# Relative-position-bias softmax: the first two chunks loaded in pieces on two DMA queues

## The chip, the cores and the metric

The kernel runs on one core of a Trainium2 chip. The metric is the time of one execution on the device in microseconds (us); the median of several runs is compared. Before the change it is 1325.94 us (three runs, 1325.74 to 1336.57).

## What is computed

```python
# logits: (B=2, H=8, S=2112, S) fp32, rel_bias: (H, 33) fp32, max_rel = 16
rel_clipped = np.clip(pos[:, None] - pos[None, :], -max_rel, max_rel) + max_rel
bias = rel_bias[:, rel_clipped]
logits = logits + bias[None, :, :, :]
logits = logits - logits.max(axis=-1, keepdims=True)
exp = np.exp(logits)
return (exp / exp.sum(axis=-1, keepdims=True)).astype(np.float32)
```

Each row of 2112 numbers gets a bias that depends only on the head and on the clipped distance to the diagonal, and then a softmax. Input and output are 285.5 MB each, so 571 MB pass between the chip's main memory (HBM) and the core's own memory (SBUF).

## The kernel before, in words

One batch has 8 x 2112 = 16,896 rows, which is 132 (`RP`) for each of the 128 partitions. A **chunk** is 6 (`R`) rows of each partition, 128 x 12,672 fp32 numbers or 6.49 MB (6336 KB on the page). There are four chunk buffers, `X[0]` to `X[3]` (`NBUF = 4`): `X[0]` and `X[1]` carry two neighbouring groups of rows of batch 0, `X[2]` and `X[3]` the same groups of batch 1. The outer loop has 11 (`K`) turns of four chunks, 44 chunks in all. Every chunk is loaded once, worked on in place and stored from the same buffer.

Three engines and two DMA queues share the work, and the order on each is written by hand:

- **SyncE** (SP) issues the loads. Four loads come first, one for each buffer (line 97). Then a loop (line 99) waits for the store of a buffer (`st[m]`) and issues the next load into it.
- **VectorE** (DVE) first builds the bias. It clears a tile (line 120), waits for the small `rel_bias` load (`rb`, line 143), spreads the 33 values of its head over a band in a PSUM tile `F` (lines 144 to 168), and then enters its loop (line 222). At the head of each turn `window(k)` copies the strip of `F` that this turn needs into `F2` (line 172). For each chunk `add(m)` waits for the chunk (`ld[m]`) and does six fused passes, one for each row: add the bias, negate, and take the running minimum (line 186). After ScalarE has done the exponentials, `scale(m)` takes reciprocals (line 210) and multiplies four of the six rows (line 213).
- **ScalarE** (ACT) issues the load of `rel_bias` (line 122) when VectorE's clearing is done (`zero`). Then it does the six exponentials of a chunk with their sums (line 197), scales the other two rows (line 218), and issues the chunk's store (line 95) when all six rows are scaled (`scaled`).

Loads so go on SyncE's queue (q1 on the page), stores and the `rel_bias` load on ScalarE's queue (q10). Both queues feed the same 16 DMA engines. GpSimd makes two small index tables at the start and nothing else; TensorE does nothing.

Of the kernel before, what the change touches and what calls it, by code (L numbers as in the profile page):

```python
# [15 lines left out]
def kernel(  # L16
# [6 lines left out]
    nc = tc.nc  # L23
    P = 128
    B, H, S, S2 = logits.shape
# [3 lines left out]
    RP = H * S // P  # L29
# [4 lines left out]
    NBUF = 4  # L34
    R = 6
    M = NBUF // B
    G = M * R
# [6 lines left out]
    X = [io.tile([P, R * S], FP32, tag=f"X{b}", name=f"X{b}") for b in range(NBUF)]  # L44
# [22 lines left out]
    def view(t, offset, dims):  # L67
        return bass.AP(tensor=t.tensor, offset=t.offset + offset, ap=[[list(t.ap[0])[0], P]] + dims)

    def rows(t, k, m):  # L70
        return bass.AP(
            tensor=t.tensor, offset=t.offset + (m // M) * (H * S * S) + (m % M) * R * S + k * (G * S), ap=[[RP * S, P], [1, R * S]],
        )

    with tc.tile_critical(no_gpsimd_drain=True):  # L75
        ld = [nc.alloc_semaphore(f"ld{b}") for b in range(NBUF)]
        st = [nc.alloc_semaphore(f"st{b}") for b in range(NBUF)]
# [2 lines left out]
        scaled = nc.alloc_semaphore("scaled")  # L80
        inv = nc.alloc_semaphore("inv")
        rb = nc.alloc_semaphore("rb")
        zero = nc.alloc_semaphore("zero")
        idx = nc.alloc_semaphore("idx")
        dve = nc.alloc_semaphore("dve")

        def take(eng, sem, n):
            eng.wait_ge(sem, n).then_inc(sem, -n)  # L88

        def load(k, m):  # L90
            nc.sync.dma_start(out=X[m][:, :], in_=rows(logits, k, m)).then_inc(ld[m], 16)

        def store(k, m):
            take(nc.scalar, scaled, R)
            nc.scalar.dma_start(out=rows(out, k, m), in_=X[m][:, :]).then_inc(st[m], 16)

        for m in range(NBUF):
            load(0, m)
        with nc.Fori(0, K - 1, 1, engines=[ENG.SP]) as k:
            for m in range(NBUF):  # L100
# [5 lines left out]
        v = nc.vector  # L106
# [6 lines left out]
        def settle():  # L113
# [9 lines left out]
            out=bass.AP(tensor=F2.tensor, offset=F2.offset, ap=[[Q * step, P // Q], [1, H * W]]),  # L123
            in_=bass.AP(tensor=rel_bias.tensor, offset=rel_bias.offset, ap=[[0, P // Q], [1, H * W]]),
        ).then_inc(rb, 16)
        nc.gpsimd.iota(pid[:, :], pattern=[[0, 2]], base=0, channel_multiplier=1).then_inc(idx, 1)
        nc.gpsimd.iota(
            num, pattern=[[1, NB + 1]], base=0, channel_multiplier=0,
# [11 lines left out]
        for o, n, s, op in ((eq, NB, q, ALU.is_equal), (lt, NB, q, ALU.is_lt), (hsel, H, h, ALU.is_equal),  # L140
# [24 lines left out]
                           in_=view(reg, 1, [[1, NB - 1], [0, RP - W]])))  # L165
# [5 lines left out]
        def window(k):  # L171
            then(v.tensor_copy(out=F2[:, 0:SW], in_=F[:, bass.ds(RP - G - k * G, SW)]))  # L172
            settle()

        def row(m, i):
            return X[m][:, i * S : (i + 1) * S]

        def col(t, m, i, n=1):
            c = m * R + i
            return t[:, c : c + n]  # L180

        def add(m):
            take(v, ld[m], 16)
            for i in range(R):
                x = G - 1 - (m % M) * R - i
                v.tensor_tensor_reduce(  # L186
                    out=row(m, i), in0=row(m, i), in1=F2[:, x : x + S],
                    scale=-1.0, scalar=BIG, op0=ALU.add, op1=ALU.min, accum_out=col(nmax, m, i),
                ).then_inc(added, 1)
# [18 lines left out]
        def scale(m):  # L208
            take(v, expd, R)
            v.reciprocal(out=col(rec, m, 0, R), in_=col(tot, m, 0, R)).then_inc(inv, 1 if m < NBUF - 1 else NBUF + 1)  # L210
            scales_begin(v, m)
            for i in range(DV):
                v.tensor_scalar_mul(out=row(m, i), in0=row(m, i), scalar1=col(rec, m, i)).then_inc(scaled, 1)  # L213

        def scale_rest(m):
            scales_begin(nc.scalar, m)
            for i in range(DV, R):
                nc.scalar.activation(  # L218
                    out=row(m, i), in_=row(m, i), func=ACTF.Copy, scale=col(rec, m, i),
                ).then_inc(scaled, 1)  # L220

        with nc.Fori(0, K, 1, engines=[ENG.DVE]) as k:  # L222
            window(k)
            for m in range(NBUF):
                add(m)
                scale(m)
        with nc.Fori(0, K, 1, engines=[ENG.Activation]) as k:
            for m in range(NBUF):
                exps(m)
                scale_rest(m)  # L230
                store(k, m)
# [31 lines left out]
```

## Time and profile before

| what | before |
|---|---|
| median of three runs | 1325.94 us (1325.74, 1325.94, 1336.57) |
| span of the profiled execution | 1323.8 us; the two quick runs lie 1.9 and 2.1 us above it |
| VectorE, ScalarE busy | 866.2 us (65%), 757.2 us (57%) |
| DMA | 570.98 MB, mean 431 GB/s |
| DMA queue q1 (loads), q10 (stores) | packets take 50.0% and 49.8% of 16 engines' span |
| a chunk's load, issue to landing | 17.6 / 38.4 / 82.8 us (least, median, most) |
| a chunk's store, issue to landing | 59.0 us (median) |

The span runs from the first to the last instruction of the core. The profile gives no further time for the execution that it shows, so its own time is taken as its span and the 2.1 us by which the median run lies above it. Instruction times below are counted from the start of the span. "Issue to landing" is the time from the instruction that hands a transfer to its queue until its semaphore has fired; it contains the time for which the transfer stood behind others. An engine name with a q (SPq, ACTq, DVEq) is that engine's instruction sequencer, where waits and DMA issues sit.

### The profile page before, as it was taken

How to read it: one execution, taken by the hardware profiler on the slowest of the kernel's cores; microseconds unless marked ns; L12 is line 12 of the kernel's file. 1: busy time of each engine (PE TensorE's matmuls, PEld its weight loads, DVE VectorE, ACT ScalarE, POOL GpSimd, SP SyncE). 2: the span in 40 equal slices, each digit the busy share in tenths (PEclk: the TensorE clock that was granted, in tenths of full speed). 3: DMA queues.
4: the chain of work that ended last, by engine and by line, in shares of the span. 5: the costliest groups of instructions: out<-in, count | busy, mean ns of one | idle time of the engine just before them, and what ended most of it. 6: DMA issues, size and time to landing. Idle time of an engine off the chain costs nothing. (4 is left out here: it accounts for less than half of the span.)

```text
span 1323.8 us, 2109 instructions
## 1 busy us (share of the span) xinstructions
DVE 866.2 (65%) x781; ACT 757.2 (57%) x627; POOL 0.4 (0%) x6
## 2 busy tenths in 40 slices
DVE  6886666566766675576667666556766576566662
ACT  3776655556666555555656555555666565555663
POOL 0000000000000000000000000000000000000000
DMA  9999999999999999999999999999999999999998
GB/s 417 417 423 435 441 435 423 441 438 421 440 441 427 430 441 435 424 440 438 424 437 440 437 423 440 440 421 438 441 432 426 441 437 423 440 440 423 437 441 369
DMA packets 12682, 570.98 MB, mean 431 GB/s; under 512 B 1412, under 2 KB 1416, under 8 KB 1416
## 3 DMA queue, kind: packets, MB, share of 16 engines
q1 hardware_dynamic: 6336, 285.48, 50.0%
q10 hardware_dynamic: 6344, 285.48, 49.8%
q14 instruction: 2, 0.02, 0.0%
HBM read 285.48 MB, written 285.47 MB: 431 GB/s over the span
## 5 line engine op out<-in xcount | busy, mean ns | idle before, releaser
L197 ACT ACTIVATE X<-X,nmax 128x2112 f32<-128x2112 f32 x264 | 542.6, 2055 | 505.1 <-DVE nmax L186 472.4
L186 DVE CUSTOM_DVE_ANT_0 X<-X,F 128x2112 f32<-128x2112 f32 x264 | 605.2, 2354 | 319.1 <-DVEq L88 319.1
L213 DVE TENSOR_SCALAR X<-X,rec 128x2112 f32<-128x2112 f32 x176 | 220.3, 1315 | 2.8
L218 ACT ACTIVATE X<-X,rec 128x2112 f32<-128x2112 f32 x88 | 176.1, 2048 | 17.2 <-DVE rec L210 12.2
L210 DVE RECIPROCAL rec<-tot 128x6 f32<-128x6 f32 x44 | 8.4, 191 | 106.2 <-DVEq L88 106.2
L197 ACT ACTIVATION_READ_ACCUMULATOR X<-X,nmax 128x1 f32 x264 | 49.2, 186 | 0.0
L197 ACT ACT_TABLE_LOAD x11 | 14.1, 1283 | 22.6 <-ACTq L88 19.9
L172 DVE COPY F<-F 128x2123 f32 x11 | 26.0, 2361 | 0.5 <-DVEq L88 0.5
L186 DVE DVE_READ_ACCUMULATOR2_ANT nmax<- 128x1 f32 x264 | 21.6, 82 | 0.0
L144 DVE LOAD_MASK_SELECT F<-F x1 | 0.0, 14 | 6.2 <-DMA F<-in_rel_bias_dram 6.2
L164 DVE COPY F<-own 128x1485 f32<-128x1485 f32 x1 | 1.7, 1698 | 0.0
L120 DVE MEMSET F<- 128x264 f32 x1 | 0.3, 278 | 1.1 <-SPq L75 1.1
L142 DVE TENSOR_SCALAR Z<-rec,Z 128x16 f32<-128x16 f32 (+2 forms) x5 | 0.8, 233 | 0.1
L163 DVE TENSOR_TENSOR F<-F,own 128x528 f32<-128x528 f32 x1 | 0.7, 717 | 0.1
L160 DVE TENSOR_TENSOR F<-Z,own 128x528 f32<-128x528 f32 x1 | 0.7, 705 | 0.0
L150 DVE TENSOR_REDUCE own<-F 128x33 f32<-128x264 f32 x1 | 0.6, 609 | 0.1
L147 DVE TENSOR_TENSOR F<-F,Z 128x264 f32<-128x264 f32 x1 | 0.4, 429 | 0.1
L144 DVE STREAM_SHUFFLE F<-F 128x264 f32<-128x264 f32 x1 | 0.4, 442 | 0.0
L158 DVE SCALAR_TENSOR_TENSOR own<-Z,own 128x16 f32<-128x16 f32 x1 | 0.2, 235 | 0.2 <-DVEq L88 0.2
L155 DVE TENSOR_SCALAR own<-Z,own 128x16 f32<-128x16 f32 x1 | 0.2, 235 | 0.2 <-DVEq L88 0.2
L166 DVE COPY F<-own 128x115 f32<-128x115 f32 x1 | 0.3, 271 | 0.0
L168 DVE COPY F<-own 128x115 f32<-128x115 f32 x1 | 0.3, 271 | 0.0
(11 smaller groups left out, 1.6 us busy)
## 6 DMA issues: line engine op xcount, KB each, us to landing
X<-in_logits_dram SPq DMA_DIRECT2D x44, 6336.0 KB, 38.4
out_dram<-X ACTq DMA_DIRECT2D x44, 6336.0 KB, 59.0
F<-in_rel_bias_dram ACTq DMA_DIRECT2D x1, 4.1 KB
```

What stands on the lines that cost most here:

```text
L142: then(v.tensor_scalar(out=o, in0=num[:, 0:n], scalar1=s, scalar2=None, op0=op))
L144: then(v.stream_shuffle(out=T, in_=T, mask=[0] * Q))
L150: then(v.tensor_reduce(out=rbK, in_=view(F2, H * W, [[1, W], [W, H]]), axis=mybir.AxisListType.X, op=ALU.add))
L160: then(v.tensor_tensor(out=bands, in0=view(eq, 0, [[1, NB], [0, W]]), in1=view(rbK, W - 1, [[0, NB], [-1, W]]), op=ALU.mult))
L163: then(v.tensor_tensor(out=bands, in0=bands, in1=view(rest, 0, [[1, NB], [0, W]]), op=ALU.add))
L164: then(v.tensor_copy(out=view(F, C0 + W, [[RP, NB - 1], [1, RP - W]]), in_=view(reg, 1, [[1, NB - 1], [0, RP - W]])))
L172: then(v.tensor_copy(out=F2[:, 0:SW], in_=F[:, bass.ds(RP - G - k * G, SW)]))
L186: v.tensor_tensor_reduce(out=row(m, i), in0=row(m, i), in1=F2[:, x : x + S], scale=-1.0, scalar=BIG, op0=ALU.add, op1=ALU.min, accum_out=c ...
L197: nc.scalar.activation(out=row(m, i), in_=row(m, i), func=ACTF.Exp, scale=-1.0, bias=col(nmax, m, i), accum_out=col(tot, m, i),).then_inc( ...
L210: v.reciprocal(out=col(rec, m, 0, R), in_=col(tot, m, 0, R)).then_inc(inv, 1 if m < NBUF - 1 else NBUF + 1)
L213: v.tensor_scalar_mul(out=row(m, i), in0=row(m, i), scalar1=col(rec, m, i)).then_inc(scaled, 1)
L218: nc.scalar.activation(out=row(m, i), in_=row(m, i), func=ACTF.Copy, scale=col(rec, m, i),).then_inc(scaled, 1)
```

## The change

Only the first load of `X[0]` and of `X[1]` changes. Each is cut into two pieces, by rows of each partition:

| piece | rows of the chunk | queue | semaphore |
|---|---|---|---|
| chunk 0, first half | 0 to 2 | SyncE | `ld[0]` |
| chunk 0, second half | 3 to 5 | ScalarE, behind `rel_bias` | `head0` |
| chunk 1, first part | 0 to 4 | ScalarE, behind the piece above | `ld[1]` |
| chunk 1, last row | 5 | SyncE, between chunk 0's half and chunk 2 | `head1` |

VectorE waits for `head0` once, ahead of its loop and so ahead of the first `window` copy, and before every `add(1)` for `head1`, which stays at 16 once it is there. All other loads and all stores are as before.

```diff
+    def part(t, k, m, a, b):
+        return bass.AP(
+            tensor=t.tensor, offset=t.offset + (m // M) * (H * S * S) + ((m % M) * R + a) * S + k * (G * S),
+            ap=[[RP * S, P], [1, (b - a) * S]],
+        )
...
+        head0 = nc.alloc_semaphore("head0")
+        head1 = nc.alloc_semaphore("head1")
...
+        def load_part(eng, m, a, b, sem):
+            eng.dma_start(out=X[m][:, a * S : b * S], in_=part(logits, 0, m, a, b)).then_inc(sem, 16)
...
-        for m in range(NBUF):
+        HALF = R // 2
+        load_part(nc.sync, 0, 0, HALF, ld[0])
+        load_part(nc.sync, 1, R - 1, R, head1)
+        for m in range(2, NBUF):
             load(0, m)
...
         ).then_inc(rb, 16)
+        load_part(nc.scalar, 0, HALF, R, head0)
+        load_part(nc.scalar, 1, 0, R - 1, ld[1])
...
         def add(m):
             take(v, ld[m], 16)
+            if m == 1:
+                v.wait_ge(head1, 16)
...
+        v.wait_ge(head0, 16)
         with nc.Fori(0, K, 1, engines=[ENG.DVE]) as k:
             window(k)
```

What the change moves is seen at three places. ScalarE's instructions from its first DMA to its first exponential, before (F_62 is the tile F2; X_58 to X_61 are the four chunk buffers):

```order
L122 DMA F_62<-in_rel_bias_dram 4x264 [waits zero]
L88 UNCONDITIONAL_BRANCH
L227 UNCONDITIONAL_BRANCH
L197 ACT_TABLE_LOAD
L197 ACTIVATE X_58,tot<-X_58,nmax 128x2112 [waits added] x6
```

and now:

```order
L136 DMA F_62<-in_rel_bias_dram 4x264 [waits zero]
L102 DMA X_58<-in_logits_dram 128x6336
L102 DMA X_59<-in_logits_dram 128x10560
L96 UNCONDITIONAL_BRANCH
L246 UNCONDITIONAL_BRANCH
L215 ACT_TABLE_LOAD
L215 ACTIVATE X_58,tot<-X_58,nmax 128x2112 [waits added] x6
```

Two load pieces now stand between the `rel_bias` load and ScalarE's table load, and wait for nothing of their own. SyncE's issues ahead of its loop, and the first of the loop, before:

```order
L91 DMA X_58<-in_logits_dram 128x12672
L91 DMA X_59<-in_logits_dram 128x12672
L91 DMA X_60<-in_logits_dram 128x12672
L91 DMA X_61<-in_logits_dram 128x12672
L99 UNCONDITIONAL_BRANCH
L91 ISA [waits st0]
L91 DMA X_58<-in_logits_dram 128x12672
```

and now:

```order
L102 DMA X_58<-in_logits_dram 128x6336
L102 DMA X_59<-in_logits_dram 128x2112
L99 DMA X_60<-in_logits_dram 128x12672
L99 DMA X_61<-in_logits_dram 128x12672
L113 UNCONDITIONAL_BRANCH
L99 ISA [waits st0]
L99 DMA X_58<-in_logits_dram 128x12672
```

The first two issues have shrunk to three rows and one row; the rest stands as it stood. VectorE from the last piece of the bias to the first add, before:

```order
L168 COPY F<-own 128x115
L222 UNCONDITIONAL_BRANCH [waits dve]
L222 ISA
L172 ISA
L172 COPY F_62<-F 128x2123
L186 ISA X_58,nmax<-X_58,F_62 128x2112 [waits dve,ld0]
```

and now:

```order
L184 COPY F<-own 128x115
L241 UNCONDITIONAL_BRANCH [waits dve,head0]
L241 ISA
L188 ISA
L188 COPY F_62<-F 128x2123
L204 ISA X_58,nmax<-X_58,F_62 128x2112 [waits dve,ld0]
```

The window copy (L172, now L188) has moved behind a wait for a load of chunk 0; before, only the first add waited for that chunk.

## The prediction, made before the changed kernel was run

> **What bounds the kernel now.** I read the page's busy lines and DMA lines first, then busy time by stretches, then the first 90 us and the last 45 us of the timeline.
>
> ```profile
> span 1323.8 us, 2109 instructions
> ...
> DVE 866.2 (65%) x781; ACT 757.2 (57%) x627; POOL 0.4 (0%) x6
> ...
> DMA  9999999999999999999999999999999999999998
> GB/s 417 417 423 435 441 435 423 441 438 421 440 441 427 430 441 435 424 440 438 424 437 440 437 423 440 440 421 438 441 432 426 441 437 423 440 440 423 437 441 369
> DMA packets 12682, 570.98 MB, mean 431 GB/s; under 512 B 1412, under 2 KB 1416, under 8 KB 1416
> ...
> q1 hardware_dynamic: 6336, 285.48, 50.0%
> q10 hardware_dynamic: 6344, 285.48, 49.8%
> ...
> HBM read 285.48 MB, written 285.47 MB: 431 GB/s over the span
> ```
>
> No compute engine passes 65%, while the DMA line shows 9 in 39 of 40 slices. The packets of the two queues fill 50.0% + 49.8% = 99.8% of the 16 engines' span. So DMA sets the time, as long as one of the two queues has something to move.
>
> Four stretches and what was moved in them (columns: length, busy time of DVE, ACT and POOL with instruction counts, TensorE clock, DMA share, GB/s):
>
> ```profile
> 18.60:40.40 21.80, 19.23 (x18) 16.89 (x14) 0.00 (x0) 1.00 1.01 438
> 40.40:62.00 21.60, 19.15 (x18) 16.89 (x14) 0.00 (x0) 1.00 0.96 394
> ...
> 84.00:1260.00 1176.00, 770.58 (x680) 677.19 (x561) 0.00 (x0) 1.00 1.00 434
> ...
> 1320.00:1323.80 3.80, 0.00 (x0) 0.00 (x0) 0.00 (x0) 1.00 0.03 13
> ```
>
> From 18.6 to 40.4 us only loads are on the way, at 438 GB/s; in the long mixed stretch it is 434 GB/s. One queue alone thus moves as much as two together. A chunk is 285.48 MB / 44 = 6.488 MB, which at 434 GB/s is 14.95 us. All 88 chunk transfers need 570.98 MB / 434 GB/s = 1315.6 us, and the span is 1323.8. So **all that any edit of the order can win is 8.2 us, 0.6%**. The rows say where it lies: in the last 3.8 us next to nothing is moved (0.03), and the stretch in which the first store enters shows 394 GB/s, 21.6 x (1 - 394 / 434) = 2.0 us lost; the rest is at the start. The change touches neither the end nor the fact that a first store enters a stream of loads, so I leave these losses as they are.
>
> The adds' group (busy, mean ns of one | idle before them, releaser):
>
> ```profile
> L186 DVE CUSTOM_DVE_ANT_0 X<-X,F 128x2112 f32<-128x2112 f32 x264 | 605.2, 2354 | 319.1 <-DVEq L88 319.1
> ```
>
> VectorE's 319.1 us ahead of the adds are waits released on line 88, most of them on a chunk's load: compute is late because data is, not the other way round. A few us more or less there cost nothing while the queues stay full.
>
> **The change part by part.** The start of the timeline (start, length, instruction, idle time before it):
>
> ```profile
> 0.97 75.20 SPq L91 DMA_DIRECT2D X<-in_logits_dram  x5
> ...
> 1.40 1.12 ACTq L122 DMA_DIRECT2D F<-in_rel_bias_dram  x1
> ...
> 9.01 0.01 DVE L144 LOAD_MASK_SELECT F<-F  x1 [6.22 <-DMA F<-in_rel_bias_dram]
> ...
> 15.02 0.27 DVE L168 COPY F<-own 128x115 f32<-128x115 f32 x1
> 15.79 2.37 DVE L172 COPY F<-F 128x2123 f32 x1 [0.50 <-DVEq L88]
> 18.71 2.36 DVE L186 CUSTOM_DVE_ANT_0 X<-X,F 128x2112 f32<-128x2112 f32 x1 [0.56 <-DVEq L88]
> ...
> 21.12 2.06 ACT L197 ACTIVATE X<-X,nmax 128x2112 f32<-128x2112 f32 x1 [17.16 <-DVE nmax L186]
> ...
> 40.05 2.35 DVE L186 CUSTOM_DVE_ANT_0 X<-X,F 128x2112 f32<-128x2112 f32 x1
> 40.38 0.38 ACTq L95 DMA_DIRECT2D out_dram<-X  x1
> ```
>
> and the loads' own rows:
>
> ```profile
> L91 SPq DMA_DIRECT2D X<-in_logits_dram x44: 332/333/549, 1.0 to 1244.2; - x44
> ...
> DMA to landing us min/median/max: 17.6/38.4/82.8
> ```
>
> *When chunk 0 is complete.* Before, its load is issued at 0.97 and lands 17.6 us later (the least value; only the first load has nothing ahead of it), at 18.6 us. That is 14.95 us of data and 2.65 us of cold start. Now the first half (7.5 us of data) goes first on SyncE's queue. The second half is issued behind the `rel_bias` issue, which ends at 1.40 + 1.12 = 2.5 us. The two halves share engines that were already moving at full rate, so together they take what the whole took. Some of chunk 1's last row (one row is 14.95 / 6 = 2.5 us) slips in, because SyncE's queue is done with its half before ScalarE's is. Bounds: 18.6 us if nothing slips in, 21.1 us if the whole row does. SyncE is ahead by some 2 to 4 us, and its small packets then alternate with three times larger ones, so I take 19.3 us, near the lower bound.
>
> *The wait for `head0`.* The window copy stood at 15.79 us, before chunk 0 had landed; now it stands behind `head0`. The bias itself, released by `rel_bias` at 9.01 and ending with the copy at 15.02 + 0.27 us, is not later than before, so `head0` comes last. The first add then starts at 19.3 + 2.37 (copy) + 0.56 (the gap before the add) = 22.2 us and not 18.71: **3.5 us later** (bounds 2.8 and 5.3). Queued behind this wait are all adds; behind them ScalarE's exponentials, and so the first store. It moves from 40.38 to 43.9 us.
>
> *What that delays.* The rows around the second store, and SyncE's first issue of its loop:
>
> ```profile
> 61.37 2.35 DVE L186 CUSTOM_DVE_ANT_0 X<-X,F 128x2112 f32<-128x2112 f32 x1
> 61.69 0.34 ACTq L95 DMA_DIRECT2D out_dram<-X  x1
> ...
> 85.36 2.36 DVE L186 CUSTOM_DVE_ANT_0 X<-X,F 128x2112 f32<-128x2112 f32 x1 [2.58 <-DVEq L88]
> ```
>
> ```profile
> 75.83 180.15 SPq L91 DMA_DIRECT2D X<-in_logits_dram  x7
> ```
>
> The first four loads are 4 x 14.95 = 59.8 us of data, so at 43.9 us there are still some 18 us of loads to move. DMA stays full and the 3.5 us are hidden; without that cover they would cost 3.5 us. During those 3.5 us the loads have the engines alone, so the fourth load, whose wait ends at 85.36 us in the row above, lands 3.5 us earlier, at 81.9. The first store lands 3.5 us later and with it the fifth load is issued at 79.3 instead of 75.83. The reserve of SyncE's queue falls from 85.36 - 75.83 = 9.5 us to 2.6 us, just about a cold start. If it runs dry for a moment, ScalarE's queue still holds stores (the second is issued at 65.2, long before the first has landed) and the engines go on; each such moment moves stores ahead and gives the loads their reserve back. I cost it at 0; from above it is one uncovered cold start, 2.65 us.
>
> *Chunk 1.* Its last row goes with the end of chunk 0, its other five rows (12.5 us) share the engines with chunk 2. It lands between 33.5 us (0.97 + 2.65 + 29.9, nothing of chunk 2 first) and 48.5 us (all of chunk 2 first); by turns, some 38 us. The second add, at 40.05 before, is due at 43.6. If the worst bound held, VectorE would lose 5 us, and the second store would be issued at 70 us, still before the first has landed. Cost 0. The wait for `head1` is met from then on.
>
> *The pieces themselves.* Two more transfers are 2 x 144 packets (6336 / 44 for each load) on top of 12,682. From below they cost nothing. From above: the fastest slice shows 441 GB/s, at which a chunk takes 14.71 us, so all that packets add to a chunk is at most 0.24 us, 0.5 us for two transfers. I take 0.2 us. ScalarE's two issues (0.38 us for such a one at 40.38) stand in its wait of 17.16 us before the first exponential (the row at 21.12): cost 0.
>
> The Trainium skill, "DMA: Bandwidth & Descriptors", section "Anatomy of one DMA — SWDGE (gpsimd) path", gives a transfer a fixed 2.0 us beside its bytes at 436 GB/s. It fits transfers issued by GpSimd; taken for these queues, two more transfers would be 4.0 us (an estimate from that page) and the time 1330.1. The trace speaks against paying it in series: a chunk takes 14.95 us and not the 16.9 us of that formula.
>
> *The end.* The last add of a chunk, the last store's issue, the landing of the last stores, and SyncE's wait for them:
>
> ```profile
> 1281.59 2.36 DVE L186 CUSTOM_DVE_ANT_0 X<-X,F 128x2112 f32<-128x2112 f32 x1 [8.54 <-DVEq L88]
> ...
> 1303.34 0.34 ACTq L95 DMA_DIRECT2D out_dram<-X  x1
> ```
>
> ```profile
> DMA to landing us min/median/max: 19.3/41.8/60.5
> ```
>
> ```profile
> L88 SPq EVENT_SEMAPHORE  x44: 17/17/17, 75.6 to 1322.7; - x44
> ```
>
> The last store lands 19.3 us after its issue; 14.95 + 2.65 = 17.6 us are its own, so it stood some 1.7 us behind the store before it. DMA has no hole there now. Loads that run 3.5 us further ahead make this reserve 5.2 us: the last load lands near 1278 us, the last store is issued near 1300, and waits longer. Nothing is won, since the bytes are the same; had the first store come more than 1.7 us *earlier*, a hole would open here.
>
> **Sum.** Against the profiled execution: 1323.8 + 0.2 + 0 (later first store, hidden) + 0 (reserve) = 1324.0 us of span; the median run lies 2.1 us above the span of before, so **1326.1 us**.
>
> **The rivals.**
>
> *Each piece pays a cold start.* If the two added transfers leave the engines idle for 2.65 us each, the time is 1326.1 - 0.2 + 5.3 = 1331.2. For it: the first load's 17.6 us show that such a start exists. Against: the other queue has packets to move in every one of these moments, and with 88 transfers one behind the other the DMA line stays at 9. The Trainium skill's fixed cost above is the same rival at a lower price.
>
> *The load queue runs dry at every turn: slower.* With a reserve of 2.6 us against a cold start of 2.65, every one of the 40 later loads could start cold. Loads are half the traffic, so half of each start would be lost: 40 x 1.33 = 53 us, 1379 us. It decides where the first add is more than (9.5 - 2.65) / 2 = 3.4 us later, and I expect 3.5: the point is reached. Against it stands that a dry load queue lets the stores run ahead, which lets the next loads be issued sooner, so that the state mends itself after one or two turns.
>
> *Cold starts get shorter.* Two queues that start side by side might hide the first 2.65 us: 1323.5. For it: 8.2 us of the span are more than the bytes need. Against: the second queue's issue only ends near 3 us.
>
> *One queue was the limit, not the engines: faster.* If two queues load at twice the rate, the first 60 us shrink by up to 30: 1296 us. Against: 438 GB/s with one queue, 434 with two. This is also the case in which the change would do what its cut suggests, having chunk 0 in sooner; in the forecast it does not.
>
> **How the numbers follow.** Chances: forecast 0.75, pieces with cold starts 0.10, shorter cold start 0.09, dry load queue 0.04, queue limit 0.02. The predicted time is the forecast's. The range, 1323.3 to 1331.2, takes in the forecast with its bounds (up to 2.65 + 0.5 us more), the shorter start and the cold pieces, and leaves out 0.06. One per cent, 13 us, is about what a measurement of this kernel tells from no change, since runs of the same kernel read 1325.74 and 1336.57. Faster by over 1% is the queue limit alone, 0.02; slower the dry queue, 0.04; the rest, 0.94, is within 1%.
>
> **What would show it right or wrong.** Right: DMA at 9 in every slice but the last; the window copy starting at 19 to 21 us and the first add at 22 to 24; the first store issued near 44 us; the fourth chunk's add without a wait for its load; the last load in near 1278 us and the last store landing 22 to 24 us after its issue; a span of 1324. Wrong: a slice below 9 in the first 100 us, adds that wait longer by a us or more in every turn, or a first add before 19 us.

## The result, and the profile after

The change takes **1335.53 us** (median of 8 runs, 1331.24 to 1341.54) against 1325.97 us before (8 runs, 1325.36 to 1336.57). The ratio is 1.0068, with a 95% interval of 1.0042 to 1.0094: slower by 0.7%. The prediction was 1326.1 with a range of 1323.3 to 1331.2. So "within 1%" was right, and the time lies outside the range. Runs of one kernel differ here by up to 13 us, with a granted clock of 1.0 in all of them, so the least and the most are given beside each median. Of the change's eight runs four lie at 1331 to 1334 us and four at 1337 to 1342; the profiled one (1339.29) is of the upper four. Its span is 1337.5 us, 13.7 more than that of before, where the medians are 9.6 us apart.

The page of the changed kernel, the same lines as before:

```profile
span 1337.5 us, 2111 instructions
...
DMA  9999999999999999999999999999999999999996
GB/s 403 407 405 429 432 435 431 434 434 431 435 435 435 429 434 435 429 437 432 437 434 434 432 431 429 431 435 431 437 431 434 427 435 432 437 435 434 435 432 277
...
q10 hardware_dynamic: 6632, 294.13, 50.9%
q1 hardware_dynamic: 6336, 276.83, 48.3%
```

The byte counts of the queues have moved by the pieces (8.65 MB from q1 to q10). The DMA line reads 9 in 39 slices, as before, but its last slice is 6 and not 8 and moves 277 GB/s and not 369; the first three slices have fallen from 417, 417, 423 to 403, 407, 405. The loss is at both ends of the program and hardly to be seen in the busy digits.

The start, by the timeline (start, length, instruction, idle time before it):

```profile
20.12 2.37 DVE L188 COPY F<-F 128x2123 f32 x1 [6.11 <-DMA X<-in_logits_dram]
22.80 2.36 DVE L204 CUSTOM_DVE_ANT_0 X<-X,F 128x2112 f32<-128x2112 f32 x1 [0.31 <-DVEq L96]
...
44.48 0.39 ACTq L106 DMA_DIRECT2D out_dram<-X  x1
...
86.79 2.35 DVE L204 CUSTOM_DVE_ANT_0 X<-X,F 128x2112 f32<-128x2112 f32 x1
```

The window copy starts at 20.12 us, released by a load of chunk 0, and the first add at 22.80; the first store is issued at 44.48, and the fourth chunk's add has no wait. All this is as it was forecast. Now the first add of the fifth chunk, whose load is the first of SyncE's loop, after and then before, and SyncE's waits on the stores (first and last):

```profile
121.46 2.36 DVE L204 CUSTOM_DVE_ANT_0 X<-X,F 128x2112 f32<-128x2112 f32 x1 [10.86 <-DVEq L96]
```

```profile
115.27 2.36 DVE L186 CUSTOM_DVE_ANT_0 X<-X,F 128x2112 f32<-128x2112 f32 x1 [6.10 <-DVEq L88]
```

```profile
L96 SPq EVENT_SEMAPHORE  x44: 17/17/17, 84.3 to 1336.4; - x44
```

SyncE gets past the first store at 84.3 us (75.6 before), and the fifth chunk's add starts at 121.46 instead of 115.27: **6.2 us late**. The sixth chunk's add comes 29.9 us later, at 151.35, as in the kernel before, so this loss is taken once.

The end, with the landing times of the stores (least, median, most):

```profile
1298.23 2.36 DVE L204 CUSTOM_DVE_ANT_0 X<-X,F 128x2112 f32<-128x2112 f32 x1 [8.64 <-DVEq L96]
...
1319.99 0.34 ACTq L106 DMA_DIRECT2D out_dram<-X  x1
```

```profile
DMA to landing us min/median/max: 16.4/54.5/62.4
```

The last add starts at 1298.23, not at 1281.59: **16.6 us late**. Of these, 6.2 were there at the fifth chunk; the other 10.4 came in small steps, nearly all of them (0.1 to 1.4 us each) between the ninth and the 35th chunk. The last store lands 16.4 us after its issue instead of 19.3, so it has nothing in front of it: 2.9 us of the lateness are covered, and 16.6 - 2.9 = 13.7 us are what the span of this execution has grown by.

What DMA moved at the start and the end, after and then before (columns: length, DVE, ACT, POOL busy with instruction counts, clock, DMA share, GB/s):

```profile
0.00:110.00 110.00, 86.58 (x92) 69.51 (x58) 0.44 (x6) 1.00 0.99 408
...
55.00:80.00 25.00, 21.77 (x21) 20.22 (x19) 0.00 (x0) 1.00 0.99 379
...
1300.00:1310.00 10.00, 10.00 (x11) 8.84 (x9) 0.00 (x0) 1.00 0.91 395
1310.00:1320.00 10.00, 7.20 (x7) 8.05 (x6) 0.00 (x0) 1.00 0.14 61
```

```profile
0.00:110.00 110.00, 87.25 (x92) 70.12 (x58) 0.44 (x6) 1.00 0.99 420
...
55.00:80.00 25.00, 21.29 (x20) 20.19 (x18) 0.00 (x0) 1.00 0.97 422
...
1300.00:1310.00 10.00, 3.11 (x3) 2.07 (x2) 0.00 (x0) 1.00 0.94 406
1310.00:1320.00 10.00, 0.00 (x0) 0.00 (x0) 0.00 (x0) 1.00 0.94 406
```

The first 110 us moved 408 GB/s instead of 420, which is 110 x (1 - 408 / 420) = 3.1 us. Most of it lies between 55 and 80 us: 25 x (1 - 379 / 422) = 2.5 us. The engines were no less busy there (0.99 against 0.97), so they did not wait; what they had in hand took longer. From 1310 to 1320 us the engines moved 61 GB/s where they moved 406 before: a hole of some 8 us ahead of the last store, in which a share of 0.14 is about two engines of 16 still at work.

### The profile page after: what moved, and what is told of

Same layout as the page of the kernel before. It is cut to its first block, busy times and chain, and to the rows that moved or that the text cites. A ratio compares the mean times of both kernels' runs of the same rounds, so it can differ in the third digit from the quotient of the medians.

```text
span 1337.5 us, 2111 instructions
## 1 busy us (share of the span) xinstructions
DVE 866.2 (65%) x781; ACT 757.2 (57%) x627; POOL 0.4 (0%) x6
## 3 DMA queue, kind: packets, MB, share of 16 engines
q1 hardware_dynamic: 6336, 276.83, 48.3%
## 5 line engine op out<-in xcount | busy, mean ns | idle before, releaser
L231 DVE TENSOR_SCALAR X<-X,rec 128x2112 f32<-128x2112 f32 x176 | 220.3, 1315 | 2.8
L188 DVE COPY F<-F 128x2123 f32 x11 | 26.0, 2363 | 6.1 <-DMA X<-in_logits_dram 6.1
## 6 DMA issues: line engine op xcount, KB each, us to landing
X<-in_logits_dram SPq DMA_DIRECT2D x42, 6336.0 KB, 43.9
```

## The experiments

The table gives, from each profiled execution, the start of the first, the fifth and the last chunk's adds and the rate in the first 110 us, and from all timed runs the median, the least and most, and how many lay above 1329 us. The kernel before, which ran beside them, had 42 of 125 runs above 1329, from 5 of 24 in one group of experiments to 14 of 31 in another. The ratios in the text compare each kernel with the kernel before as it ran beside it, over all runs; they are not quotients of the medians in the table.

| run | first add | fifth chunk | last chunk | GB/s, first 110 us | median (least to most) | above 1329 |
|---|---|---|---|---|---|---|
| before | 18.71 | 115.27 | 1281.59 | 420 | 1325.97 (1325.36 to 1336.57) | 2 of 8 |
| the change | 22.80 | 121.46 | 1298.23 | 408 | 1335.53 (1331.24 to 1341.54) | 8 of 8 |
| e1 split, no gate | 19.84 | 114.16 | 1292.42 | 420 | 1336.18 (1332.13 to 1336.69) | 10 of 10 |
| e2 gate, no split | 21.47 | 114.26 | 1292.72 | 420 | 1336.41 (1328.1 to 1338.77) | 9 of 10 |
| e3 pieces, one queue | 21.42 | 112.09 | 1286.16 | 420 | 1330.63 (1325.52 to 1336.75) | 7 of 10 |
| e4 chunk 0 only | 30.73 | 118.81 | 1292.07 | 420 | 1335.94 (1325.96 to 1336.26) | 8 of 10 |
| t2 change, tail in pieces | 22.94 | 122.10 | 1291.16 | 404 | 1331.88 (1330.05 to 1340.26) | 10 of 10 |
| t1 before, tail in pieces | 18.61 | 115.11 | 1283.89 | 420 | 1326.02 (1325.69 to 1337.22) | 3 of 10 |
| before, again | 18.66 | 115.16 | 1281.69 | 420 | 1325.69 (one run) | 0 of 1 |
| o1 batch order | 18.73 | 115.20 | 1281.75 | 420 | 1326.43 (1325.29 to 1337.44) | 3 of 10 |
| s1 gate and delay, no split | 22.64 | 120.24 | 1293.90 | 409 | 1332.93 (1329.84 to 1337.36) | 10 of 10 |
| s2 change, later | 25.46 | 117.52 | 1290.79 | 421 | 1331.08 (1326.22 to 1338.5) | 6 of 10 |
| s3 chunk 1 only | 32.11 | 120.20 | 1292.01 | 420 | 1335.54 (1327.04 to 1336.92) | 8 of 10 |
| t3 no gate, tail in pieces | 19.69 | 114.15 | 1292.54 | 420 | 1336.97 (1328.94 to 1338.29) | 9 of 10 |
| j4 change, even bias | 23.09 | 121.87 | 1294.24 | 404 | 1334.24 (1331.06 to 1342.86) | 10 of 10 |
| j2 no gate, even bias | 20.16 | 114.53 | 1292.98 | 420 | 1336.5 (1325.71 to 1336.92) | 7 of 10 |
| j3 before, even bias | 18.67 | 116.03 | 1292.00 | 421 | 1328.28 (1325.97 to 1336.04) | 4 of 10 |
| j5 gate, even bias | 21.70 | 113.42 | 1281.73 | 421 | 1331.31 (1325.71 to 1337.46) | 5 of 10 |

In the change, t2, s1 and j4 a run lies above 1329 us for the slower start alone (404 to 409 GB/s), so for these four the last column does not tell how often the loads fell behind later.

### First four: which part of the change?

"The gate" is here the wait that holds the first window copy until chunk 0 has landed.

**e1, the split without the gate.**

```diff
-        v.wait_ge(head0, 16)
         with nc.Fori(0, K, 1, engines=[ENG.DVE]) as k:
...
             take(v, ld[m], 16)
+            if m == 0:
+                v.wait_ge(head0, 16)
```

> The four pieces and their queues stay as in the change; only the wait for head0 moves from ahead of the first window copy into add(0), so that the copy no longer stands behind chunk 0. Theory A (the late first store: the first add is 4.1 us later, so the first store lands late, the load queue runs dry before the fifth load, and the loads end late): the first add starts at 19.5 to 20.5 us instead of 22.80, the fifth chunk's add near 117 instead of 121.46, and the time is 1326 to 1329 us. Theory B (the pieces on two queues: the 16 DMA engines leave the first two chunks out of step, and each later transfer ends with its slowest engine): the first add moves as in A, but the fifth chunk's add stays at 119 or later, the chunks keep falling behind, and the time stays at 1332 to 1338 us.

Measured: ratio 1.0041 (1.0018 to 1.0064). The first add came at 19.84 and the fifth chunk's at 114.16, earlier even than before's 115.27. That is against theory B; but the time did not follow, and that is against theory A. The last chunk's add and the end, in stretches of 5 us:

```profile
1292.42 2.36 DVE L206 CUSTOM_DVE_ANT_0 X<-X,F 128x2112 f32<-128x2112 f32 x1 [8.47 <-DVEq L96]
```

```profile
1300.00:1305.00 5.00, 5.00 (x5) 4.74 (x5) 0.00 (x0) 1.00 0.91 395
1305.00:1310.00 5.00, 2.44 (x4) 4.33 (x5) 0.00 (x0) 1.00 0.10 41
1310.00:1315.00 5.00, 3.94 (x4) 2.91 (x2) 0.00 (x0) 1.00 0.07 30
1315.00:1320.00 5.00, 0.00 (x0) 0.00 (x0) 0.00 (x0) 1.00 1.13 487
```

The last load is 10.8 us late though the fifth was in time. From 1305 to 1315 us the DMA share is 0.10 and 0.07: one of 16 engines is 0.06. So nearly all engines wait, with one or two still at work, until the last store is issued.

**e2, the gate without the split.**

```diff
+        v.wait_ge(ld[0], 16)
         with nc.Fori(0, K, 1, engines=[ENG.DVE]) as k:
```

> The kernel before, whole loads on SyncE's queue, with one thing of the change: VectorE waits for chunk 0 ahead of the first window copy, so the first add starts near 21.5 us, 2.8 us later than before. Theory A: the fifth chunk's add comes 3 to 6 us later than before's 115.27, and the time is 1330 to 1335 us. Theory B: the delay is hidden, the chunks keep a period of 29.9 us, and the time is 1325.5 to 1327 us.

Measured: ratio 1.0053 (1.0027 to 1.0079). The fifth chunk was in time (114.26), against theory A; the time was high all the same, against theory B, with loads whole and on one queue. Both theories fall in the form they were given.

**e3, all pieces on SyncE's queue.**

```diff
         load_part(nc.sync, 0, 0, HALF, ld[0])
+        load_part(nc.sync, 0, HALF, R, head0)
+        load_part(nc.sync, 1, 0, R - 1, ld[1])
         load_part(nc.sync, 1, R - 1, R, head1)
...
-        load_part(nc.scalar, 0, HALF, R, head0)
-        load_part(nc.scalar, 1, 0, R - 1, ld[1])
```

> The four pieces with their semaphores and the wait for head0 as in the change, but all four are issued on SyncE's queue, in the order of their rows; ScalarE's queue carries only rel_bias and the stores, as before. The first add starts near 21.5 us. Theory A: as late a first store as in the run with the gate alone, so the same time as that, 1330 to 1335 us. Theory B: no second load queue, engines in step, 1325.5 to 1327 us. If the smaller pieces themselves cost (a cold start each), it is 1331 or more also where the gate alone shows 1326.

Measured: ratio 1.0000 (0.9967 to 1.0032), runs from 1325.52 to 1336.75. The least time is that of before, so the pieces have no price of their own. Between A and B it does not decide.

**e4, only chunk 0 cut.**

```diff
-        load_part(nc.sync, 1, R - 1, R, head1)
-        for m in range(2, NBUF):
+        for m in range(1, NBUF):
...
-        load_part(nc.scalar, 1, 0, R - 1, ld[1])
...
-            if m == 1:
-                v.wait_ge(head1, 16)
```

> Only chunk 0 is cut, its second half on ScalarE's queue as in the change and with the wait for head0 ahead of the window; chunk 1 is one whole load on SyncE's queue. Theory A: first add near 22.8 us as in the change, so the same time, 1332 to 1338 us. Theory B, where the five-row piece of chunk 1 that shares the engines with chunk 2 sets the engines apart: 1326 to 1329 us; where the halves of chunk 0 already do it: 1332 to 1338 us.

Measured: ratio 1.0033 (1.0004 to 1.0063). The first add, and the sixth chunk's (145.18 before):

```profile
30.73 2.36 DVE L199 CUSTOM_DVE_ANT_0 X<-X,F 128x2112 f32<-128x2112 f32 x1 [0.31 <-DVEq L95]
```

```profile
144.59 2.36 DVE L199 CUSTOM_DVE_ANT_0 X<-X,F 128x2112 f32<-128x2112 f32 x1 [4.36 <-DVEq L95]
```

The half on ScalarE's queue took its turns against whole loads, so the first add came 12.0 us late, three times as late as in the change, which none of the expectations had. Yet the sixth chunk is 0.6 us *earlier* than before and the first 110 us moved 420 GB/s. **A late first store costs nothing up to there by its lateness alone**, as the prediction said. The time is in theory A's range, but A's way to it, a late start that stays, is not what this run shows: the last chunk is 10.5 us late all the same, and all of that comes after the sixth.

### Four on the end and on the addresses

**t2, the change with its last chunk in pieces.** The last turn is written out, and its last chunk is scaled and stored in pairs of rows. In the code `one(i)` is VectorE's add of row i, `two(i)` its reciprocals and scaling of rows i and i + 1 (so VectorE scales all six rows of this chunk), `ex(i)` ScalarE's exponential of row i, and `out2(i)` the store of rows i and i + 1:

```diff
+            for i in range(4):
+                one(i)
+            two(0)
+            one(4)
+            one(5)
+            two(2)
+            two(4)
...
+            for i in range(4):
+                ex(i)
+            out2(0)
+            ex(4)
+            ex(5)
+            out2(2)
+            out2(4)
```

> The change as it is, but the last of the 44 chunks is worked and stored in three pieces of two rows: VectorE scales rows 0 and 1 after the fourth add, rows 2 and 3 after the sixth, then rows 4 and 5, and ScalarE stores each pair at once. So the first third of the last store is issued some 12 us after the last load lands instead of 22. Theory D (the time of the change is lost at the end: the last load lands some 16 us later than before, which is more than the queue of stores covers, so the DMA engines stand idle for about 10 us ahead of the last store): most of that hole is filled and the time falls by 6 to 10 us from the change's 1335.5, to 1326 to 1330 us, though the last load is as late as before. Rival E (the engines lose the time evenly, by slower transfers on the way): no more than 2 us are won, 1333 us or more.

Measured: 1331.88 us, ratio to before 1.0029 (1.0000 to 1.0059). That is between what D (1326 to 1330) and E (1333 or more) expected.

```profile
0.00:110.00 110.00, 86.45 (x92) 69.38 (x58) 0.44 (x6) 1.00 0.99 404
1300.00:1310.00 10.00, 9.93 (x12) 6.72 (x8) 0.00 (x0) 1.00 0.98 426
1310.00:1320.00 10.00, 2.87 (x4) 0.00 (x0) 0.00 (x0) 1.00 0.98 422
```

The hole is gone (422 GB/s from 1310 to 1320 instead of 61). What stays is the loss at the start, 404 GB/s, and with it 1329.7 us of span. In this execution the loads fell behind by little after the fifth chunk (6.8 us late there, 9.6 at the last), so part of the gain over the change is that and not the pieces.

**t1, the kernel before with the same end.** The same edit, on the kernel before.

> The kernel before with the same last chunk in three pieces of two rows. Theory D: in the runs in which before shows 1326 the last store has no hole ahead of it, so nothing is won there (1325 to 1327 us); in those that show 1329 to 1337 the hole is filled. The spread of the runs shrinks and the median is 1325 to 1328 us. Rival E: the same spread as before's own runs, 1326 to 1337 us.

Measured: 1326.02 us, ratio 1.0016 (0.9984 to 1.0047). The usual runs did not move, as D has it. But three of ten runs lay at 1335 to 1337, so the spread did not shrink, as rival E has it. D names at most a part of the loss.

**o1, chunks in the order batch 0, 1, 0, 1.**

```diff
-            tensor=t.tensor, offset=t.offset + (m // M) * (H * S * S) + (m % M) * R * S + k * (G * S), ap=[[RP * S, P], [1, R * S]],
+            tensor=t.tensor, offset=t.offset + (m % B) * (H * S * S) + (m // B) * R * S + k * (G * S), ap=[[RP * S, P], [1, R * S]],
...
-                x = G - 1 - (m % M) * R - i
+                x = G - 1 - (m // B) * R - i
```

> The kernel before with the chunks of a turn in another order: batch 0, batch 1, batch 0, batch 1 instead of 0, 0, 1, 1. Queues, sizes and instructions are the same; only the addresses of the loads relative to the stores that run beside them change. Theory F (loads are slowed where their addresses meet those of the stores on the way): the share of runs above 1328 us and the time between chunks change clearly, to nearly none (1325.5 to 1327) or to nearly all (1332 to 1338). Rival G (the slowing comes from how the engines fall out of step, whatever the addresses): the same mix as before, median 1326 to 1330 us.

Measured: 1326.43 us, ratio 1.0010 (0.9985 to 1.0035), three of ten runs above 1329: the same mix as before. Theory F, in the form of this exchange, is not borne out.

**The kernel before again.** No edit.

> The kernel before once more, for a second profile. Its own runs beside the first four experiments fall into three groups, near 1325.8, 1329.7 and 1336 us. If this execution is of the first group, its chunks have a period of 29.9 us throughout; if of the others, and theory D holds, the period is 30.1 to 30.5 us in the middle third and the last load lands 5 to 12 us later than 1281 us, as in the runs with the change's parts.

Measured: 1325.69 us, a period of 29.9 us from the fifth chunk on and the last add at 1281.69: an execution of the usual kind, which says that the profile of before was no exception, and nothing on the late runs.

### Four on the start and on the late engine

**s1, gate and a further delay, no split.**

```diff
+        v.wait_ge(ld[0], 16)
+        then(v.tensor_copy(out=F2[:, 0:850], in_=F[:, 0:850]))
+        settle()
         with nc.Fori(0, K, 1, engines=[ENG.DVE]) as k:
```

> No split: the kernel before with the gate (VectorE waits for chunk 0 ahead of the first window copy) and one further copy of 850 columns behind it, so that the first add starts near 22.8 us, as late as in the change. Theory H (the loss in the change's first 110 us, 408 GB/s instead of 420 and the fifth add 6 us late, comes from the moment at which the first store enters): the first 110 us show 408 GB/s, the fifth add starts at 120 us or later, the fastest runs are 1330 or more. Theory I (it takes the pieces on two queues as well): 420 GB/s, the fifth add at 113 to 116 us, the fastest runs at 1326 to 1328.

Measured: ratio 1.0037 (1.0015 to 1.0058), no run under 1329.84. The first 110 us and the fifth chunk:

```profile
0.00:110.00 110.00, 87.77 (x93) 69.67 (x58) 0.44 (x6) 1.00 0.99 409
```

```profile
120.24 2.36 DVE L186 CUSTOM_DVE_ANT_0 X<-X,F 128x2112 f32<-128x2112 f32 x1 [9.81 <-DVEq L88]
```

Without any split, the loss of the change is there: 409 GB/s, the fifth chunk 5.0 us late. All it took was a first add at 22.64 us.

**s2, the change with a later first add.**

```diff
         v.wait_ge(head0, 16)
+        then(v.tensor_copy(out=F2[:, 0:2123], in_=F[:, 0:2123]))
+        settle()
```

> The change with one more copy of 2123 columns ahead of the loop, so the first add starts near 25.7 us instead of 22.8 and the first store is issued near 47.4. Theory H, with the moment of the first store deciding: the loss changes, either gone (420 GB/s in the first 110 us, fastest runs 1326 to 1328) or larger. Theory I: as in the change, 404 to 410 GB/s in the first 110 us, fastest runs 1330 to 1332. The plain view, that each us of delay of the first store costs its us: 3 us more than the change.

Measured: 1331.08 us, ratio 1.0012 (0.9976 to 1.0047), four of ten runs under 1327.

```profile
0.00:110.00 110.00, 86.28 (x92) 68.84 (x57) 0.44 (x6) 1.00 0.99 421
```

```profile
117.52 2.36 DVE L204 CUSTOM_DVE_ANT_0 X<-X,F 128x2112 f32<-128x2112 f32 x1 [4.27 <-DVEq L96]
```

With the split and a first add 2.7 us *later* than in the change the loss at the start is gone (421 GB/s), and the least time falls from 1331.24 to 1326.22. Theory H holds against I and against the plain view: the moment decides, not the pieces and not the delay as such. The four kernels with a first add between 22.6 and 23.1 us (the change, t2, s1, j4), whose first store is issued at 44.3 to 44.8 us, show 404 to 409 GB/s in the first 110 us, 369 to 381 between 55 and 80 us, and no run under 1329.8. All others, with first adds at 18.6 to 21.7 and at 25.5 to 32.1 us, show 420 or 421, and 422 to 444 between 55 and 80 us. Each of these rates is from one profiled execution.

**s3, only chunk 1 cut.** Chunk 0 whole on SyncE's queue, the gate on its semaphore, chunk 1 as in the change.

```diff
-        HALF = R // 2
-        load_part(nc.sync, 0, 0, HALF, ld[0])
+        load(0, 0)
...
-        load_part(nc.scalar, 0, HALF, R, head0)
...
-        v.wait_ge(head0, 16)
+        v.wait_ge(ld[0], 16)
```

> Chunk 0 is one whole load on SyncE's queue and VectorE waits for it ahead of the first window copy; only chunk 1 is cut, five rows on ScalarE's queue and one on SyncE's, as in the change. The two queues then work on chunk 0 and chunk 1 at the same time, so chunk 0 lands late, near 30 us, and the first add starts near 33. Theory I with the five-row piece as the cause: 404 to 412 GB/s in the first 110 us. If neither piece alone does it (chunk 0's halves alone showed 420), 420 GB/s, and then what costs is the two together or the moment.

Measured: ratio 1.0043 (1.0015 to 1.0072); first add at 32.11 as expected, 420 GB/s in the first 110 us. The five-row piece is not the cause of the loss at the start either; the last load is 10.4 us late, as in e1, e2 and e4.

**t3, no gate, the last chunk in pieces.** The edits of e1 and t2 together.

> The split without the gate, whose ten runs were all 1332 to 1337 us with the last load 10.8 us late and a hole ahead of the last store, now with the last chunk worked and stored in three pieces of two rows. Theory D (those 10 us are the hole at the end): 1325.5 to 1329 us for nearly all runs. If it stays at 1332 to 1337, the hole is not what costs, and the DMA engines lose the time on the way.

Measured: 1336.97 us, ratio 1.0064 (1.0038 to 1.0091): nothing won over e1. Theory D's price for the hole is refuted here. The last 25 us in stretches of 5:

```profile
1310.00:1315.00 5.00, 4.24 (x5) 1.23 (x2) 0.00 (x0) 1.00 0.70 297
1315.00:1320.00 5.00, 0.00 (x0) 0.00 (x0) 0.00 (x0) 1.00 1.00 426
1320.00:1325.00 5.00, 0.00 (x0) 0.00 (x0) 0.00 (x0) 1.00 0.59 250
1325.00:1330.00 5.00, 0.00 (x0) 0.00 (x0) 0.00 (x0) 1.00 0.07 30
1330.00:1334.70 4.70, 0.00 (x0) 0.00 (x0) 0.00 (x0) 1.00 0.04 18
```

The store pieces are there in time, and from 1315 to 1320 us all engines move 426 GB/s. Then they finish one after the other, and from 1325 us on the share is 0.07 and 0.04: about **one engine of 16** is still moving what was its part all along. As far as the packet counts tell, all engines have the same to do (6336 / 16 = 396 packets on q1), so this one is some 10 us behind the others: they stop near 1323 us (0.59 of 5 us), it near 1333 (0.04 x 16 x 4.7 = 3 us after 1330). The waits in the code are for 16 increments of a transfer's semaphore, and the trace has 16 landings for each whole transfer, so every chunk is as late as its latest engine. Read so, the hole of e1 is the other engines' idle time, and the late engine sets the end.

The times of these 16 landings show the engines drift apart on the way. In the kernel before, the first and the last landing of a store are 1.9 to 4.2 us apart, all through. In e1 they are 1.0 us apart for the first store, 3.0 for the 11th and 22.6 for the 30th, whose last landing comes 15.1 us after the last but one; and between the 11th and the 31st chunk the adds go from 0.5 to 10.9 us late. So the lag of one engine grows while the loads fall behind. In j3, below, the landings come to lie 22 us apart too, but the last is never more than 4.1 us behind the last but one, so there more than one engine lags. What makes an engine slow is not shown.

### Four on the cause of the late engine

**j4, j2, j3, j5: the rel_bias load spread evenly**, in the change, in e1, in the kernel before and in e2.

```diff
-            out=bass.AP(tensor=F2.tensor, offset=F2.offset, ap=[[Q * step, P // Q], [1, H * W]]),
-            in_=bass.AP(tensor=rel_bias.tensor, offset=rel_bias.offset, ap=[[0, P // Q], [1, H * W]]),
+            out=bass.AP(tensor=F2.tensor, offset=F2.offset, ap=[[8 * step, 16], [1, H * W]]),
+            in_=bass.AP(tensor=rel_bias.tensor, offset=rel_bias.offset, ap=[[0, 16], [1, H * W]]),
```

> The change, with the rel_bias load spread over 16 partitions, eight apart, instead of 4: each of the 16 DMA engines should carry one small row of it, not four engines one each. Theory J (one engine falls behind because four of the engines have one more packet ahead of the load pieces on ScalarE's queue, so that their turns between the queues differ): no straggler, period of 29.9 us for all chunks, 1326 to 1329 us, or 1330 if the loss near the first store stays. Rival K (what falls behind is set by the moment of the first store and by chance on the way, not by rel_bias): 1331 to 1341 us as the change.

> The split without the gate (ten runs of 1332 to 1337 us, last load 10.8 us late), with the rel_bias load spread over 16 partitions. Theory J: most runs at 1325.5 to 1328 us, last load near 1281 us. Rival K: 1332 to 1337 us again.

> The kernel before, with the rel_bias load spread over 16 partitions. Theory J: its runs lose their upper groups (1329 to 1337 us), all at 1325.3 to 1327. Rival K: the same mix as before's, some 60 to 80 per cent near 1326 and the rest up to 1337.

> The kernel before with the gate (nine of ten runs of 1335 to 1339 us), with the rel_bias load spread over 16 partitions. Theory J: most runs at 1325.5 to 1328 us. Rival K: 1335 to 1338 us again.

Measured: 1.0042 (1.0013 to 1.0071), 1.0030 (0.9996 to 1.0063), 1.0013 (0.9989 to 1.0036) and 1.0023 (0.9990 to 1.0057). Late runs stay in all four: 10, 7, 4 and 5 of ten above 1329. In j2 and j5 they are fewer than in e1 (10) and e2 (9), 12 of 20 against 19 of 20; but the two pairs ran on different chips and at different times, so this does not decide whether the even load helps a little. Theory J, as the cause, does not hold: late runs stay, and j2's last chunk is 11.4 us late. j3's profile is of use for another reason: it caught a late execution of what is nearly the kernel before. Its first and its last chunk's add:

```profile
18.67 2.36 DVE L186 CUSTOM_DVE_ANT_0 X<-X,F 128x2112 f32<-128x2112 f32 x1 [0.36 <-DVEq L88]
```

```profile
1292.00 2.36 DVE L186 CUSTOM_DVE_ANT_0 X<-X,F 128x2112 f32<-128x2112 f32 x1 [8.64 <-DVEq L88]
```

The start is that of before to 0.04 us, and the last load is 10.4 us late, as in e1, e2, e4 and s3. So the falling behind does not need the change; the kernel before has it too, more or less, in 42 of 125 runs by their times. e1, e2, e4 and s3, each a part of the change, have it in eight to ten of ten runs; of the change itself the upper four of eight runs show it clearly.

## Why the prediction was wrong, point by point

**Right.** Compute set nothing: chunk 0 was whole at about 20 us (forecast 19.3), the first add came at 22.80 (22.2), the first store was issued at 44.48 (43.9), the fourth chunk's add had no wait, and the delay of the first store was hidden in itself: with 12.0 us of it (e4) the sixth chunk was in time. Two more pieces cost nothing that could be found: the least run is 1325.52 us in e3, and 1325.71 in j2, with the pieces on both queues as in the change. That refutes the rival of cold starts. By the same runs, the fixed cost of the Trainium skill ("DMA: Bandwidth & Descriptors", section "Anatomy of one DMA — SWDGE (gpsimd) path") is not paid in series here. The load queue did run dry once: by the trace the fourth load had landed at 84.1 us, and the fifth was issued at 84.52. It did mend itself, as the period was 29.9 us from the fifth chunk to the sixth and for most of the next ones, so the rival with 53 us did not come.

**Wrong, first: "What that delays", costed at 0.** It counted bytes at a constant rate and had the fifth load issued at 79.3 us. SyncE got there at 84.3 us. The engines moved 408 GB/s and not 420 in the first 110 us, 3.1 us, most of it between 55 and 80 us and with the engines fully busy, and the fifth chunk was 6.2 us late. s1 and s2 show that this hangs on the moment at which the first store comes, a first add between 22.6 and 23.1 us, with or without a split. The row that warned of it was in the prediction: 394 GB/s where the first store enters, 2.0 us. It was taken as a constant ("I leave these losses as they are"), when the price depends on the moment. Its upper bound, one cold start of 2.65 us, was too low.

**Wrong, second: "The end", with a reserve of 5.2 us.** It let the lead that the loads have at the start last to the end, and had the last load in near 1278 us. It came near 1298. In the profiled execution the loads fell behind by another 10.4 us on the way, where the prediction had every chunk on time, and at the end of t3 and e1 one of the 16 engines, in the change some two, are seen behind the others. The reserve itself was mis-sized too: a last store with nothing in front of it took 16.4 us and not 17.6, so it had stood 2.9 us behind the store before it and not 1.7. That changes little beside 16.6 us. The prediction looked for holes common to all engines, and a DMA line of nines does not show one engine that is 10 us late.

**And the range.** It was made from one execution of before and three times, one of which (1336.57) was read as the width of a measurement. It was a sign that this kernel has runs that are 10 us longer, and the question whether the change makes them more frequent was not asked. No chance was given to it. That "within 1%" came true owes something to luck: the two losses that the prediction had at nothing add up to less than 13 us in the median.

**What stays open.** Why the first 110 us are slower for just that moment, and why an engine falls behind, and does so more often after most changes of the start. The order of the batches (o1) and the uneven `rel_bias` load (j) do not account for it. Whether something outside this core plays a part was not tested. The Trainium skill, "DMA: Bandwidth & Descriptors", section "Latency and other measured facts", says that two of a core's 16 engines, 7 and 15, are usually slower than the rest, with a guess at the cause that concerns GpSimd's transfers, of which this kernel has none. No view here names the engine that was late, so it can't be said whether it is one of them.

None of the variants is faster than the kernel before; the least ratio is e3's 1.0000.

## What to carry to other kernels

In a kernel that DMA fills from end to end, an edit of the first microseconds can't win more than the few that the engines stand idle, but it can lose more than its own size, as it did here, since it sets the moment at which the stores first meet the loads. Before costing such an edit at nothing, look at how the runs of the kernel before are spread, not only at their median: runs of more than one length, here near 1326, 1330 and 1336 us, are a warning that something small may decide between them. And to see whether a DMA-bound program ends on all its engines or on one, read the DMA share in short stretches at its end; a share near 0.06 is one of 16.

## What was not expected of the hardware

One DMA engine of 16 can end some 10 us in 1330 behind the others (share 0.07 from 1325 to 1330 us in t3), and the 16 landings of one store can come to lie 22.6 us apart (e1). The rate over the first 110 us is 404 to 409 GB/s for first adds at 22.6 to 23.1 us, and 420 to 421 for those before and after. And a piece of a load on a second queue does not get half of the engines by bytes: in e4 the half chunk, taking turns with whole loads, released the first add at 30.73 us, 7.9 us later than the same half in the change.
